# A planner with other prices, and rotary halves exchanged by copies instead of DMAs

## The chip, the cores and the metric

The kernel runs on one core of a Trainium2 chip. The metric is the device time of one execution in microseconds (us). The core has five engines that each work through their own queue in order: TensorE (PE; its weight loads are listed as PEld), VectorE (DVE), ScalarE (ACT), GpSimd (POOL) and SyncE (SP), which here issues nearly all DMAs.

## The reference: what is computed

Two layers of a decoder trunk for one sequence of 512 tokens, model width 1024, in float32. Per layer:

```python
mod = c_silu @ w_ada + b_ada                       # shift, scale, gate
u = rms_norm(x, norm_g) * (1 + scale) + shift
z = u @ w_in                                       # split into 18 column groups
ya = dsa_attention(rope(aq), rope(ak), av, rope(iq), rope(ik), iw) * silu(ag)
yb = swa_sinks_attention(rope(bq), rope(bk), bv, sinks) * silu(bg)
yc = stick_breaking_attention(cq, ck, cv) * silu(cg)
merged = sigmoid(ma)*(ya @ w_br_a) + sigmoid(mb)*(yb @ w_br_b) + sigmoid(mc)*(yc @ w_br_c)
x = x + gate * (merged @ w_out)
```

Mixer A attends to the 128 best keys by an indexer's score, mixer B to a window of 128 tokens, mixer C breaks sticks over all earlier tokens. Heads have 64 channels. The rotary step takes a head's halves x1, x2 (32 channels each) to `[x1*cos - x2*sin, x1*sin + x2*cos]`; it is applied to the queries and keys of A and B and to those of the indexer.

## The kernel before

**Tiles.** Activations lie with channels on the 128 partitions (rows) and the 512 tokens along the row. A projection tile is 128 output channels, that is two heads, by 512 tokens: one PSUM bank, filled by 24 matmuls. Each weight chunk (128x512, tile `wstage`) is split on the chip into a high part `whi` (a cast) and a low part `wlo` (a subtraction), and each activation likewise into `uh` and `ul`; of the four products three are summed, which makes 3 matmuls for each of 8 blocks of the width of 1024. Projection banks are called `ps_z` (three of them), the banks for scores, transposes and mixer outputs `ps_s` (five).

**Phases.** Per layer: a first phase (seven projection tiles, among them the indexer's `ik`, `iq0`, `iq1`), a phase for values with tokens on partitions, then a long middle in which projections, three mixers, gates and branch products are woven together, then the output projection with the next norm. VectorE selects mixer A's keys in the middle phase: 16 rounds of a maximum of eight and a replacement for each of three token blocks, on the tiles `score`. Mixer C runs first, then B, then A; A's first mask addition reads `score`.

**The rotary step** is `rope_evac` (called by `evac` for `iq`, `bq`, `bk`, `aq`, `ak`: 15 tiles per layer). It copies the finished bank z to a tile `zs` in SBUF, has SP issue four DMAs of 32 rows that write the exchanged halves to `m2` (the profile calls it `m`), multiplies z by the cosines into `zc`, multiplies `m2` by the signed sines, and adds. The results `Q` and `KH`/`klow` are then stacked and split for the score matmuls. The key tile of the indexer has a function of its own, `key_and_value`, with the same DMAs.

**Softmax of A and B.** VectorE adds the mask and takes the row maximum in eight operations (`t,mx<-ps_s`, shown as CUSTOM_DVE_ANT_0 in the trace and as ISA in the order), forms the negated maximum `nm`; ScalarE takes exponentials in eight operations with their sums (`den`); the normalised tiles are transposed on TensorE (`ps_s<-small,t`, float32 against the identity).

**What sets the order.** Every operation is first recorded, with the engines that may do it: `cast` may go to ACT, to DVE, and from SBUF to POOL as well; `both` (two tensors) to DVE or, when neither lies in PSUM, to POOL. `Recorder.price` gives each choice a `cost` (how long the engine is held) and a `lag` (until the result is there). `Recorder.forward` is a list scheduler: it gives the next free engine the ready operation with the earliest deadline, keeps a port that DVE and POOL share, hands out buffers, and counts DMAs through one channel. `Recorder.latest` works deadlines back from the end. `order` repeats this five times and keeps the plan that ends first by its own prices. `emit` writes the instructions out in that order, so that each engine's queue is fixed. All instructions are emitted in one helper, which is why nearly every row has the same line (L567 before; L577 in the changed program).

Of the kernel before, what the change touches and what calls it, by code (L numbers as in the profile page):

```python
# [25 lines left out]
F32 = mybir.dt.float32  # L26
F32R = mybir.dt.float32r
BF16 = mybir.dt.bfloat16
# [230 lines left out]
class Recorder:  # L259
    PIPE = 0.17  # L260
    CROSS = 0.055
    ROUNDS = 5

    def __init__(self, tc, nc, psum, sbuf):
# [58 lines left out]
    def price(self, x, engine, op, args, kw):  # L323

        y = Way()
        y.op, y.args, y.kw, y.mode, y.port = op, args, kw, None, False
        o = x.writes[0] if x.writes else None
        if op == "preload_act_table_set":
            y.cost = y.lag = 1.3
            return y  # L330
        if op == "dma_start":
            n = 1
            for d in (o or x.reads[0]).shape:
                n *= d
            y.cost, y.lag, y.mode = 0.35 if engine == "SP" else 0.1, n * 4 / 365e3, "dma"
            return y
        n = 1
        for d in o.shape[1:]:
            n *= d
        from_psum = any(v.tile.pool.name[:3] == "ps_" for v in x.reads)  # L340
        if engine == "PE":
            if op == "pairs":
                w = [q[2].shape[-1] for q in args]
                if args[0][2].dtype == F32:
                    c, y.mode = 0.03 + sum(4 * v / 2.4e3 for v in w[::2]), "c"
                else:
                    c, y.mode = 0.095 + sum(max(0.112, 0.4375e-3 * v + 0.007) for v in w[::2]), "r"
                y.cost, y.lag = c, c + self.PIPE
            elif op == "transpose":
                c, y.mode = 0.109, "t"  # L350
                y.cost, y.lag = c, c + self.PIPE
            else:
                rhs, y.mode = args[2], "m"
                c = 4 * n / 2.4e3 + 0.01 if rhs.dtype == F32 else 0.06 if rhs.dtype == BF16 else 0.4375e-3 * n + 0.007
                y.cost, y.lag = c, c + self.PIPE
            return y
        accum = "accum_out" in kw
        if engine == "ACT":
            b = 0.1 if isinstance(kw.get("bias"), View) or isinstance(kw.get("scale"), View) else 0.0
            c = 0.2 + 0.82e-3 * n + (b if not accum else 0.08) - (0.03 if from_psum else 0)  # L360
        elif engine == "DVE":
            y.port = not from_psum and op not in ("max", "match_replace", "memset", "reciprocal")
            if op == "tensor_tensor_scan":
                c = 1.21
            elif op == "max":
                c = 0.15 + 1.05e-3 * args[1].shape[-1]
            elif op == "match_replace":
                c = 0.145 + 1.05e-3 * args[2].shape[-1]
            elif n <= 16:
                c = 0.2 + (0.1 if accum else 0)  # L370
            elif op == "tensor_tensor_reduce":
                c = 0.147 + 1.05e-3 * n
            elif from_psum:
                c = 0.147 + 1.05e-3 * n + (0.08 if accum else 0)
            elif op in ("tensor_scalar", "tensor_copy"):
                c = 0.2 + 0.45e-3 * n if op == "tensor_scalar" else 0.15 + 0.5e-3 * n
            elif op == "memset":
                c = 0.1 + 0.6e-3 * n
            else:
                c = 0.15 + 1.05e-3 * n + (0.08 if accum else 0)  # L380
        else:
            y.port = n > 16
            if op == "memset":
                c = 0.12 if n < 16 else 0.52
            elif op == "tensor_copy":
                c = 0.2 + 0.82e-3 * n
            elif op == "tensor_scalar":
                c = 0.2 + 2.8e-3 * n
            else:
                c = 0.1 + 2.35e-3 * n  # L390
        y.cost = y.lag = c
        return y


    def forward(self):
        E = {e: {"free": 0.0, "port": 0.0, "mode": None, "ready": {}, "pend": []} for e in self.real}
        dma_free = 0.0
        waiting = {}
        for x in self.list:
            x.left, x.est, x.bound, x.taken = len(x.preds), 0.0, len(x.tiles), False  # L400
# [32 lines left out]
        while len(out) < len(self.list):  # L433
            best = None
            for name, e in E.items():
                free, port, pend, ready = e["free"], e["port"], e["pend"], e["ready"]
                while pend and pend[0][0] <= free + 1e-9:
                    i = heapq.heappop(pend)[1]
                    ready[i] = self.list[i]
                mine = None  # L440
                for i in list(ready):
                    x = ready[i]
                    if x.taken:
                        del ready[i]
                        continue
                    y = x.alts[name]
                    at = max(free, port) if y.port else free
                    if len(x.alts) > 1 and self.elsewhere(x, name, at, E):
                        continue
                    key = (at, x.prio, i)  # L450
                    if mine is None or key < mine:
                        mine = key
                if mine is None or mine[0] > free + 1e-9:
                    while pend and self.list[pend[0][1]].taken:
                        heapq.heappop(pend)
                    if pend:
                        est, i = pend[0]
                        x = self.list[i]
                        at = max(est, port) if x.alts[name].port else est
                        key = (at, x.prio, i)  # L460
                        if (mine is None or key < mine) and not (len(x.alts) > 1 and self.elsewhere(x, name, at, E)):
                            mine = key
                        elif mine is None:
                            mine = None
                if mine is not None:
                    asked = max(free, self.list[mine[2]].est)
                    if best is None or (mine[0], asked, mine) < best[:3]:
                        best = (mine[0], asked, mine, name)
            assert best is not None, "no instruction may go"
            (at, _, i), name = best[2:]  # L470
            e, x = E[name], self.list[i]
            y = x.alts[name]
            x.taken, x.engine = True, name
            e["ready"].pop(i, None)
            hold = y.cost
            if name == "PE":
                if e["mode"] is not None and y.mode != e["mode"]:
                    hold += 0.095 if {"c", "r"} & {y.mode, e["mode"]} else 0.0
                e["mode"] = y.mode
            x.start, x.hold = at, hold  # L480
            e["free"] = at + hold
            if y.port:
                E["POOL"]["port"] = at + hold + (self.CROSS if name == "DVE" else 0.0)
                E["DVE"]["port"] = at + hold
            if y.mode == "dma":
                x.end = dma_free = max(at + 1.9, dma_free) + y.lag
            else:
                x.end = at + y.lag + (hold - y.cost)
            out.append(x)
            for s in x.succs:  # L490
                s.est = max(s.est, x.end + self.between(x, s))
                s.left -= 1
                offer(s)
            for t in x.tiles:
                t.users -= 1
                t.done = max(t.done, x.end + self.CROSS)
                if t.users == 0:
                    heapq.heappush(t.pool.free, (t.done, t.slot))
                    give(t.pool)
        return max(x.end for x in out), out  # L500

    def between(self, x, s):
        if x.engine == "PE" and "PE" in s.alts:
            return x.start - x.end
        return 0.0 if list(s.alts) == [x.engine] and x.alts[x.engine].mode != "dma" else self.CROSS

    def elsewhere(self, x, name, at, E):

# [86 lines left out]
def trunk(ctx, tc, xT, vecs, w_ss, w_gt, w_first, w_t, w_v, w_br, w_o, rope, consts, out):  # L595
# [22 lines left out]
    def t512(tag, bufs=None, dt=F32):  # L618
        return rec.tile(tag, [P, S], dt)
# [213 lines left out]
        st[name] = sigmoid_from(z, t512("sm", 2))  # L833

    def rope_evac(z):
        zs, m2, zc = t512("zs"), t512("m2"), t512("zc")
        cast(zs, z)
        for a, b in ((0, 32), (32, 0), (64, 96), (96, 64)):
            SP.dma_start(m2[a:a + 32], zs[b:b + 32])
        DVE.tensor_tensor(out=zc, in0=z, in1=cos_t, op=OP.mult)  # L840
        both(m2, m2, sin_t, OP.mult)
        both(zc, zc, m2, OP.add)
        return zc
# [712 lines left out]
    for fn, chunks in wv.items:  # L1556
# [4 lines left out]
        args = [ch.get(pos - len(chunks) + i) for i in range(len(chunks))]  # L1561
# [65 lines left out]
```

## Time and profile before

| | |
|---|---|
| median of 3 runs | 1181.32 us (1180.83 to 1181.7) |
| the profiled execution | 1182.6 us, of which the span from first to last instruction is 1180.8 |
| granted TensorE clock | 0.998 |
| PE busy | 1164.9 us, 99% of the span |
| DVE busy | 940.6 us, 80% |
| ACT busy | 563.2 us, 48% |
| POOL busy | 255.5 us, 22% |
| mean DMA rate | 118 GB/s |

How to read it: busy is time in which an engine runs instructions, so the rest of the span is waiting. In a row of a group, the numbers behind the bar are total busy time and the mean in ns of one instruction, then the idle time ahead of its instructions and what ended it. In a row of waits stand the total, the number of times and the longest. Tile names come without buffer numbers.

### The profile page before, as it was taken

The numbers are of one execution on the slowest core, as the hardware profiler recorded it, in microseconds if no ns is written. First come the engines' busy times: TensorE is split into PE (matmuls) and PEld (weight loads), VectorE is DVE, ScalarE is ACT, GpSimd is POOL, SyncE is SP. The second block draws the span as 40 slices with busy tenths as digits, with TensorE's granted clock in tenths as the row PEclk, the third lists the DMA queues.
The fourth block names the chain that finished last, engine by engine and source line by source line (L and its number), as shares of the span: only waits on it lengthen the run. The fifth ranks groups of instructions, "written<-read, shape, count | busy, mean of one in ns | idle before, by whom it ended". The sixth has DMA issues, their size and how long they took to land.

```text
span 1180.8 us, 17862 instructions
## 1 busy us (share of the span) xinstructions
PE 1164.9 (99%) x6006; PEld 967.6 (82%) x6006; DVE 940.6 (80%) x2094; ACT 563.2 (48%) x1171; POOL 255.5 (22%) x297
## 2 busy tenths in 40 slices
PE   9999999999999999999999999999999999999997
PEld 8799777788878887778899987777888788877886
DVE  7867999989888788686476599998897887667754
ACT  6534677653456632642144157665534654235222
POOL 1100455531111101001210016453221011111120
PEclk9999999999999999999999999999999999999999
DMA  9644323344434454344534432234342334322342
GB/s 338 230 115 126 90 72 90 99 119 122 117 105 128 134 144 142 89 138 148 166 113 104 135 97 80 81 88 115 120 125 74 97 83 124 98 65 88 94 128 100
DMA packets 81916, 139.41 MB, mean 118 GB/s; under 512 B 10016, under 2 KB 22560, under 8 KB 81824
## 3 DMA queue, kind: packets, MB, share of 16 engines
q1 hardware_dynamic: 80672, 136.17, 39.4%
q10 hardware_dynamic: 1152, 2.10, 0.5%
q8 instruction: 47, 0.77, 0.3%
q14 instruction: 45, 0.37, 0.1%
HBM read 125.39 MB, written 4.19 MB: 110 GB/s over the span
## 4 chain that ended last, share of the span: by engine, by line
PE 89%; DVE 4%; DMA 3%; ACT 1%; SPq 1%; issue 1%; DVEq 0%; ACTq 0%
PE ps_z L567 68%; PE ps_s L567 16%; PE ps_s L565 5%; DMA wstage<-in_w_first 2%; DVE t L567 1%; SPq L567 1%; ACT t L567 1%; DMA m<-zs 1%; DVE Y L567 0%; DVE wlo L567 0%; DVE Q L567 0%; DVE m L567 0%; DMA wstage<-in_w_ss 0%; DVE zc L567 0%; DVE vc L567 0%
## 5 line engine op out<-in xcount | busy, mean ns | idle before, releaser
L567 PE MATMUL ps_z<-uh,whi 128*128 128x512 f32 (+1 forms) x908 | 356.7, 394 | 2.7 <-DVE xm L567 1.2
L567 PE MATMUL ps_z<-uh,wlo 128*128 128x512 f32 (+1 forms) x908 | 353.3, 389 | 0.0
L567 PE MATMUL ps_z<-ul,whi 128*128 128x512 f32 (+1 forms) x908 | 352.8, 389 | 0.2 <-DVE ul L567 0.2
L567 POOL TENSOR_TENSOR wlo<-wstage,whi 128x512 fp32r<-128x512 f32 (+1 forms) x135 | 172.8, 1281 | 619.2 <-DVE whi L567 312.0
L567 PEld LDWEIGHTS ps_z<-uh,whi 128*128 128x128 f32 x908 | 170.4, 188 | 38.8 <-issue 3.6
L567 PEld LDWEIGHTS ps_z<-uh,wlo 128*128 128x128 f32 x908 | 170.6, 188 | 35.5 <-issue 1.7
L567 PEld LDWEIGHTS ps_z<-ul,whi 128*128 128x128 f32 x908 | 170.8, 188 | 32.6 <-DVE ul L567 0.9
L567 DVE TENSOR_TENSOR wlo<-wstage,whi 128x512 fp32r<-128x512 f32 (+2 forms) x237 | 154.5, 655 | 13.2 <-ACT whi L567 4.9
L567 ACT CAST whi<-wstage 128x512 fp32r<-128x512 f32 (+2 forms) x148 | 87.7, 596 | 153.2 <-PE ps_z L567 103.2
L567 DVE CAST whi<-wstage 128x512 fp32r<-128x512 f32 (+2 forms) x172 | 70.3, 409 | 105.9 <-PE ps_z L567 88.1
L567 PE MATMUL ps_z<-Y,whi 128*128 128x512 f32 x384 | 118.8, 390 | 0.8 <-ACT e L567 0.8
L567 ACT ACTIVATE e<-ps_z 128x512 f32<-128x512 f32 x68 | 40.3, 594 | 124.9 <-PE ps_z L567 124.7
L567 PEld LDWEIGHTS ps_z<-Y,whi 128*128 128x128 f32 x384 | 71.7, 188 | 16.0 <-issue 1.1
L567 ACT ACTIVATE e<-e 128x512 f32<-128x512 f32 x96 | 60.3, 630 | 39.2 <-DVE e L567 38.1
L567 ACT ACTIVATE t<-t 128x512 f32<-128x512 f32 x120 | 71.7, 628 | 8.5 <-POOL t L567 3.4
L567 PE MATMUL ps_z<-Y,wlo 128*128 128x512 f32 x192 | 74.6, 389 | 0.0
L567 ACT ACTIVATE t<-t,nm 128x256 f32<-128x256 f32 (+3 forms) x128 | 65.1, 510 | 16.2 <-DVE nm L567 16.2
L567 POOL CAST whi<-wstage 128x512 fp32r<-128x512 f32 (+2 forms) x52 | 31.4, 605 | 177.9 <-PE ps_z L567 104.3
L567 PE MATMUL ps_s<-small,t 128*128 128x128 f32 x432 | 57.7, 273 | 1.6 <-DVE t L567 0.9
L567 PEld LDWEIGHTS ps_s<-small,t 128*128 128x128 f32 x432 | 50.0, 140 | 10.5 <-ACT t L567 1.6
L567 DVE MAX8 m<-score 128x8 f32<-128x256 f32 (+2 forms) x96 | 53.4, 556 | 1.7
L567 DVE SCALAR_TENSOR_TENSOR wstage<-wstage,csr 128x512 f32<-128x512 f32 x64 | 46.2, 723 | 10.1 <-DMA wstage<-in_w_ss 7.2
(209 smaller groups left out, 2019.6 us busy)
## 6 DMA issues: line engine op xcount, KB each, us to landing
wstage<-in_w_t SPq DMA_DIRECT2D x212, 256.0 KB, 2.7
wstage<-in_w_v SPq DMA_DIRECT2D x48, 182.0 KB, 2.3
Y<-in_w_ss SPq DMA_DIRECT2D x16, 512.0 KB, 6.4
m<-zs SPq DMA_DIRECT2D x128, 64.0 KB, 2.0
wstage<-in_w_gt SPq DMA_DIRECT2D x32, 256.0 KB, 2.7
wstage<-in_w_ss SPq DMA_DIRECT2D x32, 256.0 KB, 2.8
wstage<-in_w_o SPq DMA_DIRECT2D x32, 256.0 KB, 2.7
wstage<-in_w_first SPq DMA_DIRECT2D x16, 256.0 KB, 4.6
```

What stands on the lines that cost most here:

```text
L565: self.real[engine].matmul(*[real(a) for a in q[:3]], start=q[3], stop=True, skip_group_check=True)
L567: made = getattr(self.real[engine], y.op)(*[real(a) for a in y.args], **{k: real(v) for k, v in y.kw.items()})
```

## The change

Two things. First, `rope_evac` has no `zs` and no DMAs any more: four copies of 32 rows read the bank z in PSUM and write `m2` at the exchanged rows. Each may go to ScalarE or VectorE. `key_and_value` stays as it was. Second, the planner's constants are others: how long operations take by engine and shape, how much of one is overlapped by the next on its engine (`OVERLAP`), what TensorE's changes between kinds of matmul cost (`ENTER`), when the port shared by DVE and POOL comes free, how long until a dependent instruction may start (`between`), how long DMAs take to issue and land, and how many may be under way (`LANES`).

```diff
 class Recorder:
     PIPE = 0.17
     CROSS = 0.055
+    NEXT = 0.033
+    LANES = 8
+    OVERLAP = {"PE": 0.0, "ACT": 0.095, "DVE": 0.083, "POOL": 0.06, "SP": 0.0}
+    ENTER = {"m": 0.0, "t": 0.035, "c": 0.17, "r": 0.17}
+    TOPORT = 0.13
...
-            y.cost, y.lag, y.mode = 0.35 if engine == "SP" else 0.1, n * 4 / 365e3, "dma"
+            y.cost, y.lag, y.mode = (0.58 if x.reads and x.writes and not x.reads[0].tile.pool.fixed else 0.36) if engine == "SP" else 0.1, n * 4 / 385e3, "dma"
...
-                c = 4 * n / 2.4e3 + 0.01 if rhs.dtype == F32 else 0.06 if rhs.dtype == BF16 else 0.4375e-3 * n + 0.007
+                c = 4 * n / 2.4e3 + 0.01 if rhs.dtype == F32 else 0.06 if rhs.dtype == BF16 else (n + 33.5) / 2.4e3
...
-            b = 0.1 if isinstance(kw.get("bias"), View) or isinstance(kw.get("scale"), View) else 0.0
-            c = 0.2 + 0.82e-3 * n + (b if not accum else 0.08) - (0.03 if from_psum else 0)
+            b = 0.09 * sum(isinstance(kw.get(k), View) for k in ("bias", "scale"))
+            c = 0.205 + 0.83e-3 * n + (b if not accum else 0.18) - (0.04 if from_psum else 0)
...
             elif op in ("tensor_scalar", "tensor_copy"):
-                c = 0.2 + 0.45e-3 * n if op == "tensor_scalar" else 0.15 + 0.5e-3 * n
+                c = 0.225 + 0.45e-3 * n if op == "tensor_scalar" else 0.16 + 0.52e-3 * n
...
-        y.cost = y.lag = c
+        y.cost, y.lag = c - self.OVERLAP[engine], c
...
                 if e["mode"] is not None and y.mode != e["mode"]:
-                    hold += 0.095 if {"c", "r"} & {y.mode, e["mode"]} else 0.0
+                    hold += self.ENTER[y.mode]
...
             if y.port:
-                E["POOL"]["port"] = at + hold + (self.CROSS if name == "DVE" else 0.0)
-                E["DVE"]["port"] = at + hold
+                E["POOL"]["port"] = at + y.lag + self.CROSS if name == "DVE" else at + hold
+                E["DVE"]["port"] = at + y.lag - self.TOPORT
             if y.mode == "dma":
-                x.end = dma_free = max(at + 1.9, dma_free) + y.lag
+                x.end = dma_free = max(at + 3.0, dma_free) + y.lag * (1.6 if dma_free < 5.5 else 1.0)
+                lanes.append(x.end)
+                if name == "SP" and len(lanes) >= self.LANES:
+                    e["free"] = max(e["free"], lanes[-self.LANES])
...
-        return 0.0 if list(s.alts) == [x.engine] and x.alts[x.engine].mode != "dma" else self.CROSS
+        if x.alts[x.engine].mode == "dma":
+            return self.CROSS
+        return self.NEXT if list(s.alts) == [x.engine] else 0.15 if "PE" in s.alts else 0.07 if list(s.alts) == ["POOL"] else 0.04
...
     def rope_evac(z):
-        zs, m2, zc = t512("zs"), t512("m2"), t512("zc")
-        cast(zs, z)
+        m2, zc = t512("m2"), t512("zc")
         for a, b in ((0, 32), (32, 0), (64, 96), (96, 64)):
-            SP.dma_start(m2[a:a + 32], zs[b:b + 32])
+            cast(m2[a:a + 32], z[b:b + 32])
         DVE.tensor_tensor(out=zc, in0=z, in1=cos_t, op=OP.mult)
```

The other changed prices are of the same kind (matmul pairs, transposes, `match_replace`, very short operations, and 0.06 us more for `scalar_tensor_tensor`).

**The order at three places.** First VectorE around the rotary tile aq0 of layer 0. Here `zc_3693` and `m2_3700` (after the change `zc_3684` and `m2_3676`) are its two tiles, `Q_3758` (`Q_3723`) its result, and the ISA rows are the mask additions of mixer B's last pair. Before:

```order
L567 TENSOR_TENSOR zc_3693<-ps_z_3582,rt_84 128x512
L567 TENSOR_TENSOR Y_3698<-e_3685,Y_3698 128x512
L567 CAST whi_3716<-wstage_3595 128x512
L567 TENSOR_TENSOR wlo_3724<-wstage_3595,whi_3716 128x512
L567 ISA t_3734,mx_3735<-ps_s_3718,cb_85 128x256
L567 ISA mx_3735 128x1
L567 TENSOR_TENSOR m2_3700<-m2_3700,rt_84 128x512
L567 ISA t_3749,mx_3735<-ps_s_3720,cb_85 128x256
```

And in the changed program:

```order
L577 COPY m2_3676<-ps_z_3570 32x512
L577 TENSOR_TENSOR zc_3684<-ps_z_3570,rt_84 128x512
L577 TENSOR_TENSOR Y_3679<-e_3668,Y_3679 128x512
L577 TENSOR_TENSOR m2_3676<-m2_3676,rt_84 128x512
L577 TENSOR_TENSOR wlo_3699<-wstage_3503,whi_3671 128x512
L577 TENSOR_TENSOR zc_3684<-zc_3684,m2_3676 128x512
L577 ISA t_3719,mx_3720<-ps_s_3697,cb_85 128x256
```

The multiplication of `m2` and the sum now stand ahead of the first mask addition; before, the multiplication stood behind it. One of the four copies is on VectorE, the three others stand together on ScalarE.

Second GpSimd's last instructions, which split the weights of layer 1's end. Before:

```order
L567 TENSOR_TENSOR wlo<-wstage,whi 128x512 x6
L567 TENSOR_SCALAR e<-e 128x512
L567 TENSOR_TENSOR wlo<-wstage,whi 128x512
L567 CAST whi<-wstage 128x512
L567 TENSOR_TENSOR wlo<-wstage,whi 128x512 x12
```

And in the changed program:

```order
L577 TENSOR_TENSOR wlo<-wstage,whi 128x512 x2
L577 CAST whi<-wstage 128x512
L577 TENSOR_TENSOR wlo<-wstage,whi 128x512 x2
L577 CAST whi<-wstage 128x512 x2
L577 TENSOR_TENSOR xm_8673<-xm_8673,sm 128x512
L577 TENSOR_SCALAR e<-e 128x512
```

The subtractions of that end have gone to VectorE. Over the program 512-wide `wlo` go from 178 to 236 on VectorE and from 130 to 72 on GpSimd.

Third VectorE in the last update of the residual, with the squares `m` summed for the final norm. Before:

```order
L567 SCALAR_TENSOR_TENSOR xm_12111<-ps_z,mods_77,G 128x256
L567 SCALAR_TENSOR_TENSOR xm_12141<-ps_z,mods_77,G 128x256
L567 TENSOR_SCALAR xm_12111<-xm_12111,small 128x256
L567 TENSOR_TENSOR m_11865<-m_11865,e 128x256
L567 TENSOR_TENSOR t<-xm_11858,ps_s 128x256
```

And in the changed program:

```order
L577 SCALAR_TENSOR_TENSOR xm_12051<-ps_z,mods_77,G 128x256
L577 TENSOR_TENSOR m_11805<-m_11805,e 128x256
L577 SCALAR_TENSOR_TENSOR xm_12081<-ps_z,mods_77,G 128x256
L577 TENSOR_SCALAR xm_12081<-xm_12081,small 128x256
L577 TENSOR_TENSOR t<-xm_11798,ps_s 128x256
```

The sum into `m` has moved ahead of the last update.

More of the change, by code (lines that the diff above doesn't have):

```diff
@@ L344, in price @@
                 if args[0][2].dtype == F32:
-                    c, y.mode = 0.03 + sum(4 * v / 2.4e3 for v in w[::2]), "c"
+                    c, y.mode = 0.21 + sum(4 * v / 2.4e3 for v in w[::2]), "c"
                 else:
-                    c, y.mode = 0.095 + sum(max(0.112, 0.4375e-3 * v + 0.007) for v in w[::2]), "r"
+                    c, y.mode = 0.26 + sum((v + 33) / 2.4e3 for v in w[::2]), "r"
                 y.cost, y.lag = c, c + self.PIPE
             elif op == "transpose":
-                c, y.mode = 0.109, "t"
+                c, y.mode = 0.1085, "t"
                 y.cost, y.lag = c, c + self.PIPE
@@ L367, in price @@
             elif op == "match_replace":
-                c = 0.145 + 1.05e-3 * args[2].shape[-1]
+                c = 0.215 + 1.045e-3 * args[2].shape[-1]
             elif n <= 16:
-                c = 0.2 + (0.1 if accum else 0)
+                c = 0.27 if op == "tensor_scalar" and len(x.reads) > 2 else 0.22 if op == "tensor_scalar" else 0.165 + (0.1 if accum else 0)
             elif op == "tensor_tensor_reduce":
@@ L379, in price @@
             else:
-                c = 0.15 + 1.05e-3 * n + (0.08 if accum else 0)
+                c = 0.15 + 1.05e-3 * n + (0.0 if accum else 0.06 if op == "scalar_tensor_tensor" else 0.0)
         else:
@@ L396, in forward @@
         E = {e: {"free": 0.0, "port": 0.0, "mode": None, "ready": {}, "pend": []} for e in self.real}
-        dma_free = 0.0
+        dma_free, lanes = 0.0, []
         waiting = {}
```

## The prediction, made before the result was known

> **What bounds the kernel now.** I read the page's busy table first, then the chain of waits, then who TensorE waited for.
>
> ```profile
> PE 1164.9 (99%) x6006; PEld 967.6 (82%) x6006; DVE 940.6 (80%) x2094; ACT 563.2 (48%) x1171; POOL 255.5 (22%) x297
> ```
> ```profile
> 399.73 59.87 PE ps_z L567 x264
> ```
> The second row is one piece of the chain: 264 projection matmuls of 128x512 in 59.87 us, 227 ns each, with nothing between them. Busy on PE is therefore real work here, not a pipeline that looks full. The change leaves the count of matmul instructions as it is (5835 in both programs, by the order), so TensorE's own work cannot shrink. What can move is the 15.9 us of the 1180.8 us span in which it is not busy:
>
> ```profile
> PE ps_z L567 <- ACT e L567: 2.0, 2, 1.2
> PE ps_s L567 <- DVE t L567: 1.4, 3, 0.7
> PE ps_z L567 <- DVE xm L567: 1.2, 1, 1.2
> PE ps_s L567 <- DVE m L567: 1.2, 1, 1.2
> PE ps_s L567 <- DVE epst L567: 1.0, 1, 1.0
> PE ps_s L567 <- ACT t L567: 0.6, 1, 0.6
> ...
> ```
> The columns are total us, times, longest. All waits of PE sum to 8.7 us (these 7.4, and 1.3 of the first 70 us, for loads and first tiles). The other 7 us are the tail after PE's last matmul. So a gain is a matter of a few us, and only a loss could be large.
>
> **Which of these waits the rotary exchange makes.** The chain in the stretch of aq0, layer 0, in order of time:
>
> ```profile
> 327.45 0.59 ACT zs L567
> ...
> 328.62 1.43 SPq L567
> ...
> 330.73 2.05 DMA m<-zs
> ...
> 332.80 0.69 DVE m L567
> ...
> 335.16 0.69 DVE Q L567
> 335.84 0.03 issue
> 335.88 0.69 DVE Q L567
> ...
> 337.03 0.34 DVE t L567
> ...
> 338.15 1.97 ACT t L567 x8
> ```
> The copy to zs ends at 328.0; the four DMAs are issued one behind the other on SP and land at 332.8. VectorE, in order, holds the mask additions of a softmax (t) behind m, so ScalarE's exponentials start at 338.15, and PE waits 0.6 us for t. The same road leads to two more waits: in layer 1 bq1's m starts 5.5 us after the end of its zs copy, and PE waits 1.2 us for xm, queued on VectorE behind it; ak0's m starts 4.3 us after its copy, and PE waits 0.7 us for t:
>
> ```profile
> 793.37 0.61 DVE zs L567
> ...
> 799.52 0.69 DVE m L567
> ...
> 912.64 0.59 ACT zs L567
> ...
> 917.55 0.69 DVE m L567
> ```
>
> **The change part by part.**
>
> *The exchange.* Thirty rotary tiles lose one whole copy and four DMAs each and get four 32-row copies from PSUM. By the order, 85 of the 120 copies stand on ScalarE and 35 on VectorE. No 32-row copy from PSUM is in the trace; nearest are
>
> ```profile
> L567 ACT COPY zs<-ps_z 128x512 f32<-128x512 f32 x20 | 11.7, 583 | 22.9 <-PE ps_z L567 19.5 <-DVE zc L567 2.3 <-DMA m<-zs 1.1
> L567 ACT CAST KH<-KH 64x512 fp32r<-64x512 f32 x13 | 8.0, 619 | 0.5
> L567 DVE COPY zs<-ps_z x8: 678/680/692, 61.6 to 989.0; 128x512 f32<-128x512 f32 x8
> ```
> The middle one moves 64 rows to the other half and costs as much as 128 rows of its kind, so I price by row length: 0.583 us on ScalarE, 0.680 on VectorE. The lower bound would be a quarter of these (if rows counted), the upper 0.71 with the 0.03 us gap below. ScalarE: 85 less 21 whole copies, +37 us; VectorE: 35 less 9, +18 us. SP loses 120 issues. Latency: at aq0 and ak0 three copies go to ScalarE and one to VectorE beside them, 1.75 us; bq1 has all four on ScalarE, 2.3 us. From the start of the copy to the start of m it was 5.4, 4.9 and 6.2 us. Each m multiplication comes 3 to 4 us earlier; the PE waits there were 0.6, 0.7 and 1.2 us. They go: **-2.5 us** (bounds -2.5 and 0, if the next input is as late). Next late at the first place are ScalarE's eight exponentials themselves. The added copies on ScalarE are hidden by its 52% of free time; without that cover a tile's evacuation would be up to 4 x 0.58 us and hold its ps_z bank (three exist) that long.
>
> *The plan.* Prices and overlaps in the planner alter which engine takes work and its place on that engine; the matmuls keep nearly their order. The largest shift is the weight split's subtraction:
>
> ```profile
> L567 DVE TENSOR_TENSOR wlo<-wstage,whi 128x512 fp32r<-128x512 f32 x178 | 122.4, 689 | 9.8 <-ACT whi L567 3.1
> L567 DVE CAST whi<-wstage 128x512 fp32r<-128x512 f32 x139 | 58.8, 424 | 83.2 <-PE ps_z L567 70.9 <-PE ps_s L567 8.4 <-DMA wstage<-in_w_first 1.1
> L567 POOL TENSOR_TENSOR wlo<-wstage,whi 128x512 fp32r<-128x512 f32 x130 | 167.9, 1292 | 590.0 <-DVE whi L567 312.0 <-DVE score L567 97.3 <-PE ps_z L567 48.4
> ```
> 178 become 236 on VectorE and 130 become 72 on GpSimd: +58 x 0.689 = +40 us against -58 x 1.292 = -75. With 31 more whi casts (+13) and the copies (+18), VectorE gets about 70 us more, of 240 us free over the span. The free time lies mostly where it waits for PE to give weight buffers back (83.2 us ahead of whi), so at most places this costs nothing. It matters in the selection of keys, from the first replacement of maxima to the first mask of mixer A:
>
> ```profile
> core 0: us, PE busy (x) PEld busy (x) DVE busy (x) ACT busy (x) POOL busy (x), PEclk, DMA share, GB/s
> 115.00:351.80 236.80, 236.19 (x1238) 189.83 (x1237) 216.62 (x501) 140.32 (x293) 85.42 (x108) 1.00 0.35 101
> 690.00:929.00 239.00, 236.99 (x1237) 189.86 (x1237) 215.35 (x498) 140.58 (x292) 84.91 (x106) 1.00 0.34 97
> ```
> ```profile
> L567 DVE TENSOR_SCALAR t<-t,den 128x256 f32<-128x256 f32 x46 | 14.8, 354 | 0.1
> L567 DVE CUSTOM_DVE_ANT_0 t<-ps_s,cb 128x256 f32<-128x256 f32 x48 | 18.0, 418 | 0.2
> ```
> There VectorE is 91 and 90% busy, and the order puts 38 and 34 more instructions on it. On average: 9.5 wlo (+6.5), 8.5 whi (+3.6), 7.5 copies (+5.1), 6 operations of 64 rows at 0.7 us (+4.2), 7 normalisations of t fewer (-2.5): +17 us, some 16 after overlap. It would then be 98 and 97% busy. Waits that need not return are those for the exchange (m<-zs) and for weight buffers (whi<-PE):
>
> ```profile
> DVE whi L567 <- PE ps_z L567: 3.5, 4, 1.3
> DVE m L567 <- DMA m<-zs: 2.6, 2, 1.3
> ...
> DVE zc L567 <- ACT zs L567: 1.4, 3, 0.6
> ...
> ```
> ```profile
> DVE whi L567 <- PE ps_z L567: 4.5, 5, 1.5
> DVE m L567 <- DMA m<-zs: 4.4, 4, 1.5
> ...
> ```
> (layer 0, then layer 1, which has the same 1.4 us for zc). That fits, barely. New PE waits: lower bound 0, upper 17.8 us (worked out under rival B). A selection round may slide without harm as long as mixer A's mask is in time, so I take a value near the low end, **+1.5 us**.
>
> The plan now takes 0.083 us from every VectorE operation for overlap with the one before. The chain above shows both kinds: t, 0.418 us long by its group, follows at steps of 0.34, but each 64-row Q starts 0.03 us after the end of its forerunner. [...]
>
> PE's remaining mid-program waits (ACT e 2.0, and 0.7 of DVE t) come from other late inputs. A plan with nearer durations should remove some; bounds 0 and -2.7, I take two thirds, **-1.8**. The start keeps its transfers in nearly the same order: 0 (bounds 0 and -1.3). At the end the order puts the product m<-m,e ahead of the last xm update:
>
> ```profile
> 1172.18 0.42 ACT L567 ACTIVATE e<-xm 128x256 f32<-128x256 f32 x1 [0.96 <-DVE xm L567]
> 1172.80 0.70 PE L567 MATMUL ps_s<-m,nones 128*128 128x256 f32 x2 [1.17 <-DVE m L567]
> 1173.33 0.59 PE L567 MATMUL ps_s<-e,nones 128*128 128x256 f32 x2
> ```
> Then only e (ready at 1172.60) is late and its matmul starts near 1172.8 instead of 1173.33: **-0.5** (bounds -0.6 and 0).
>
> Sum: -2.5 + 1.5 - 1.8 - 0.5 = -3.3 us. The profiled execution took 1182.6 us, a span of 1180.8 and 1.8 around it, so it would take 1179.3; it lies 1.3 above the median of the runs, 1181.32. Against the median: **1178.0 us**.
>
> **The rivals.**
>
> *A*, the forecast, 1178.0 (1176 to 1181): 0.44.
>
> *B, VectorE becomes the bound in the selection of keys.* For it: 98%, and the 0.03 us gaps at changes of rows, 0.22 us per copy against what is planned, 1.8 us in each stretch. Against it: its waits shrink when work is queued. Layer 0 needs 216.6 + 16 + 1.8 = 234.4 of 236.8 us. If all its idle time stays but that for the exchange (2.6 for m, 1.4 for zc) and for buffers (3.5), 12.7 us, it is 10.3 us over; layer 1, likewise (215.4 + 16 + 1.8 + 13.3 against 239), 7.5: together 17.8. It decides once more than 2.4 us of idle per stretch must stay. Half of the excess with the gains for exchange and tail: 1181.3 - 3.0 + 8.9 = 1187 us. 0.25.
>
> *C, nearly all mid-program waits go* (8.7 less 1.0 at the first matmul and 0.7 of the last): 1174.3 us. For it: each is a single late input of at most 1.2 us. Against: the order of PE hardly alters, so the same chains stay tight. 0.18.
>
> *D, the exchange was hidden anyway*, the next input being as late: only the tail is left, 1180.8 us. For it: at the first place the exponentials follow in a chain of their own. 0.13. That the copies are not exchanged at all is excluded by the order: SP keeps 8 of 128 DMAs to m.
>
> **How the numbers follow.** The predicted time is A's. A measurement of this kernel tells about 0.2% from no change: 2.4 us, so faster is below 1179.0 and slower above 1183.7. A gives faster 0.32 and same 0.12; C faster 0.18; D same 0.13; B slower 0.20 and same 0.05. Faster 0.50, same 0.30, slower 0.20. The range, 1173 to 1188, takes in C and the middle of B; A's own is 1176 to 1181.
>
> **What would show it.** Right: no DMA to m but for the key tile, the 32-row copies at 0.58 and 0.68 us, no PE wait left behind m at the three places, VectorE near 86% of the span. B: VectorE over 97% in the two stretches and PE idle for t, Q or whi there. D: the three waits still there under another name. Wrong altogether would be a 32-row copy far from 0.6 us, or PE's busy time altered by more than 2 us.

## The result and the profile after

The changed program takes **1192.1 us** (median of 5 runs, 1191.4 to 1193.0) against 1181.7 of the kernel before on the same chip: ratio 1.009, 95% interval 1.0078 to 1.0101. It is 10 us slower; forecast were 1178 us, and 1187 for the rival in which VectorE falls behind. Of all executions in this document two stand apart, one of a later version at 2359 us and one of the kernel before at 3003 us; the ratios leave them out. The profiled execution took 1192.4 us, a span of 1190.6, 9.8 us longer than before.

The busy table on the page of the profile, after:

```profile
PE 1170.0 (98%) x6006; PEld 969.6 (81%) x6006; DVE 993.0 (83%) x2262; ACT 572.0 (48%) x1195; POOL 150.2 (13%) x195
```

TensorE's idle time in the span went from 15.9 to 20.6 us (+4.7), and its busy time, with the same 6006 matmul records, grew by 5.1. Together they are the 9.8 us. Who TensorE waited for, after (total us, times, longest):

```profile
PE ps_s L577 <- DVE t L577: 10.5, 14, 3.4
PE ps_s L577 <- DVE epst L577: 1.0, 1, 1.0
PE ps_s L577 <- DMA wstage<-in_w_first: 1.0, 1, 1.0
PE ps_s L577 <- DVE vc L577: 0.6, 1, 0.6
PE ps_s L577 <- ACT e L577: 0.2, 1, 0.2
```

The late inputs of before (ScalarE's e, 2.0 us; xm and m, 1.2 each) have all but gone. In their place TensorE waits 14 times for a tile `t` that VectorE has not yet written. The selection of keys, again from the first replacement to the first mask of mixer A, now lasts 244.1 us (236.8 before) and 241.3 (239.0 before). In the columns of the windows shown before:

```profile
117.00:361.10 244.10, 238.17 (x1231) 190.61 (x1230) 228.33 (x538) 143.33 (x304) 60.58 (x78) 0.99 0.31 90
701.70:943.00 241.30, 236.94 (x1235) 189.22 (x1234) 227.42 (x531) 143.52 (x304) 59.73 (x77) 1.00 0.31 88
```

TensorE idles 5.9 us in the first (0.6 before) and 4.4 in the second (2.0 before). VectorE is late but not full: 93.5 and 94.2%. So where does its time go? First the copies themselves, from the view of the tile `m` (count, then min/median/max in ns):

```profile
L577 ACT COPY m<-ps_z x79: 575/578/582, 64.1 to 1003.7; 32x512 f32<-32x512 f32 x79
L577 DVE COPY m<-ps_z x33: 679/684/696, 197.5 to 1001.8; 32x512 f32<-32x512 f32 x33
```

They cost what a whole copy costs, as was assumed. What was not assumed is who waits for whom. VectorE's and then ScalarE's waits for the other engine at these tiles, after:

```profile
DVE m L577 <- ACT m L577: 11.8, 18, 1.2
DVE zc L577 <- ACT m L577: 7.2, 12, 1.1
```
```profile
ACT m L577 <- DVE m L577: 19.6, 19, 2.4
ACT m L577 <- DVE zc L577: 13.9, 11, 2.9
```

A copy on ScalarE waits until VectorE's copy from the same bank has ended, `zc` on VectorE (also a read of that bank) waits for ScalarE's copy, and so on: the two engines **take turns at the bank**. None of ScalarE's 79 copies overlaps in time with any of VectorE's 61 reads of `ps_z` by `m` and `zc`. The two rows of VectorE are 19.0 us; 1.3 of them are waits of m's multiplication, which needs the copies in any case, so 17.7 us are turns. That the four copies write one tile is not what makes them wait: a little later both engines write the two halves of one tile `Q` at the same time.

```profile
335.89 0.62 ACT L577 CAST Q<-zc 64x512 fp32r<-64x512 f32 x1 [1.32 <-DVE zc L577]
...
336.23 0.42 DVE L577 CAST Q<-zc 64x512 fp32r<-64x512 f32 x1
```

What the copies and `zc` have in common is the bank. The kernel itself records no dependency between two reads, yet the waits are in the trace; no run here leaves them out. Before the change VectorE lost as much to the DMAs:

```profile
DVE m L567 <- DMA m<-zs: 19.7, 17, 2.3
...
DVE zc L567 <- ACT zs L567: 3.2, 7, 0.6
```

So the change did not free VectorE; it put one wait in the place of another. The chain in the stretch of aq0, layer 0, after, up to the longest wait of TensorE:

```profile
330.70 0.71 DVE m L577
...
331.43 0.59 ACT m L577
...
332.04 0.70 DVE zc L577
...
333.35 0.58 ACT m L577
...
333.96 0.69 DVE m L577
...
336.23 0.42 DVE Q L577
336.65 0.03 issue
336.69 0.42 DVE t L577
337.12 0.03 issue
337.15 0.70 DVE Q L577
...
347.11 0.36 DVE t L577
347.48 0.04 issue
347.52 1.76 PE ps_s L577 x7
```

The first four copies and `zc` go back and forth, and m's multiplication starts at 333.96, 3.3 us after the first copy (5.4 before the change, 1.75 forecast). The next rotary tile does the same from 340.08 (copies on VectorE and ScalarE, then `zc`). In between, each change between `Q` (64 rows) and `t` (128 rows) has the 0.03 us gap that the prediction had read off; the new plan expects an overlap of 0.083 there. Counted over all of VectorE's rows, two neighbours of 128 rows overlap by 0.082 us at the median, and where either has 64 or 32 rows there is a gap of 0.031. Some 260 such places without a wait, at 0.031 us of gap and 0.083 of overlap that is not there (a few do overlap), add up to some 25 us that the plan leaves out, 7.6 and 7.2 us of it in the two stretches. TensorE stands still for 3.4 us before 347.52, and then runs on at half speed:

```profile
335.00:343.00 8.00, 8.00 (x37) 6.64 (x37) 7.05 (x25) 2.68 (x5) 2.55 (x2) 1.00 0.26 73
347.50:352.50 5.00, 4.98 (x17) 4.16 (x18) 4.85 (x14) 2.20 (x6) 0.00 (x0) 0.50 0.04 15
```

The granted clock (third column from the end) is 0.50 in these 5 us, in which 17 matmuls run. By that clock they cost an estimated 2.5 us more, which show as busy time, not as waiting. That is half of the 5.1 us by which TensorE's busy time grew; the other half can't be put down to single rows.

### The profile page after: what moved, and what is told of

It is laid out like the page before. It is cut to its first block, busy times and chain, and to the rows that moved or that the text cites. A ratio compares the mean times of both kernels' runs of the same rounds, so it can differ in the third digit from the quotient of the medians.

```text
span 1190.6 us, 17620 instructions
## 1 busy us (share of the span) xinstructions
PE 1170.0 (98%) x6006; PEld 969.6 (81%) x6006; DVE 993.0 (83%) x2262; ACT 572.0 (48%) x1195; POOL 150.2 (13%) x195
## 4 chain that ended last, share of the span: by engine, by line
PE 79%; DVE 15%; issue 3%; ACT 2%; DMA 1%; SPq 0%; DVEq 0%; ACTq 0%
PE ps_z L577 59%; PE ps_s L577 16%; DVE t L577 6%; PE ps_s L575 4%; DVE m L577 2%; DVE score L577 2%; DVE Q L577 1%; DVE wlo L577 1%; DVE KH L577 1%; ACT m L577 1%; ACT t L577 1%; DVE klow L577 1%; DVE zc L577 1%; DMA vc<-in_xT 1%; DVE whi L577 0%
## 5 line engine op out<-in xcount | busy, mean ns | idle before, releaser
L577 DVE TENSOR_TENSOR wlo<-wstage,whi 128x512 fp32r<-128x512 f32 (+2 forms) x296 | 193.4, 656 | 13.0 <-ACT whi L577 3.6
L577 DVE CAST whi<-wstage 128x512 fp32r<-128x512 f32 (+2 forms) x213 | 86.9, 409 | 89.8 <-PE ps_z L577 73.8
L577 POOL TENSOR_TENSOR wlo<-wstage,whi 128x512 fp32r<-128x512 f32 (+2 forms) x76 | 96.8, 1277 | 507.5 <-PE ps_z L577 102.9
L577 ACT CAST whi<-wstage 128x512 fp32r<-128x512 f32 (+2 forms) x112 | 66.6, 599 | 83.1 <-PE ps_z L577 68.7
L577 ACT ACTIVATE t<-t 128x512 f32<-128x512 f32 x120 | 68.7, 625 | 10.1 <-DVE t L577 9.2
L577 PE MATMUL ps_s<-small,t 128*128 128x128 f32 x432 | 59.6, 279 | 10.6 <-DVE t L577 10.5
L577 ACT COPY m<-ps_z 32x512 f32<-32x512 f32 x79 | 45.7, 578 | 45.9 <-DVE m L577 19.6
L577 PE MATMUL ps_s<-KH,Q 128*128 128x256 f32 (+3 forms) x280 | 52.5, 309 | 0.2
```

What stands on the lines that cost most here:

```text
L577: made = getattr(self.real[engine], y.op)(*[real(a) for a in y.args], **{k: real(v) for k, v in y.kw.items()})
```

## The experiments

Two suspects, then: the turns at a bank (**T**), and the gaps at changes of rows (**H**, for held). Rivals: VectorE simply has too much work (**O**), the plan has lost slack, wherever it lay (**S**), or some other new price does it (**P**). Each ratio is to the kernel before on the same chip, with its 95% interval. Edits are against the changed program.

**One part alone.** First the new plan with the old exchange by DMA:

```diff
-        m2, zc = t512("m2"), t512("zc")
+        zs, m2, zc = t512("zs"), t512("m2"), t512("zc")
+        cast(zs, z)
-            cast(m2[a:a + 32], z[b:b + 32])
+            SP.dma_start(m2[a:a + 32], zs[b:b + 32])
```

> The changed planner with the old exchange (one whole copy and four DMAs per rotary tile). Theory T, turns: the loss comes from the exchange, since the four copies and the cosine product read one PSUM bank and the trace of the change shows ScalarE and VectorE waiting for each other there (VectorE 11.8 + 7.2 us for ScalarE's m, ScalarE 19.6 + 13.9 us for VectorE's m and zc), which the plan does not count. Then this run is near or below the kernel before: 1176 to 1183 us. Theory O, overbooked: the loss comes from the planner, which takes 0.083 us of overlap from every VectorE operation and moves 58 subtractions from GpSimd to VectorE. Then this run is as slow as the change, 1187 to 1194 us, with PE waiting for t on VectorE about 10 us.

Then the old planner (all prices and rules of before) with the new exchange:

> The old planner with the new exchange. T: slower than before, 1186 to 1194 us, with the same mutual waits of ScalarE and VectorE at m and zc. O: the old planner keeps VectorE some 8% freer, so the exchange costs nothing: 1177 to 1183 us.

Measured: the plan alone 1181.4 us, ratio 1.0001 [0.9991, 1.0010], as T expected; the copies alone 1182.3, 1.0008 [0.9998, 1.0017], as O expected. Neither costs anything; only **both together** do. VectorE's waits with the copies alone:

```profile
DVE m L567 <- ACT m L567: 14.1, 22, 1.2
DVE zc L567 <- ACT m L567: 11.5, 20, 0.9
```

25.6 us, some 24 of them turns: more than in the changed program, and no loss. The old plan charges each VectorE instruction its full duration, so it keeps room. With the new plan alone VectorE is as busy as after the change (988.1 us, 84%), fuller in the two stretches (96.5 and 95.5%), and no time is lost, which speaks against O. Nor do the gaps alone explain the loss: that program has some 21 us of them, just as unplanned. What it lacks is the turns. VectorE waits nowhere for the DMAs to `m` there, and 2.2 us for the copy `zs`:

```profile
694.60:931.30 236.70, 235.05 (x1230) 188.10 (x1228) 226.05 (x536) 133.19 (x286) 48.66 (x67) 1.00 0.33 97
```
```profile
DVE zc L577 <- ACT zs L577: 2.2, 6, 0.4
```

**All copies on ScalarE**, `ACT.copy(...)` in place of `cast(...)`:

> The change, with the four copies bound to ScalarE, so that a bank changes hands at most once, before or after the cosine product; VectorE loses 35 copies, 24 us. T: most of the mutual waits go, 1180 to 1186 us. O: VectorE is freer by 2% of the span, so also faster than the change, but the unplanned overlap remains: 1185 to 1190 us.

1187.3 us, 1.0049 [1.0034, 1.0063]: half of the loss goes. That lies in O's range and outside T's. `zc` and the copies still alternate, and VectorE also has 9.4 us less work, so this run does not part the two.

**Turns in the plan.** The planner keeps, for each PSUM tile, when each engine's last use ends, and lets a read by the other start 0.04 us after it:

```diff
+    def bank(self, x, name):
+        return max((u + 0.04 for t in x.tiles if t.pool.name[:3] == "ps_" for e, u in t.use.items() if e != name), default=0.0) if name != "PE" else 0.0
...
-                    at = max(free, port) if y.port else free
+                    at = max(max(free, port) if y.port else free, self.bank(x, name))
```

> The change, with one thing added to the planner: a read of a PSUM tile by ScalarE or VectorE may start only 0.04 us after the other engine's last read of it has ended. T: the turns are now in the plan, work is put into the gaps, and most of the loss goes: 1178 to 1184 us, with VectorE waiting for ScalarE's m less than 8 us instead of 19. O: the overbooking is untouched: 1188 to 1193 us.

1184.0 us, 1.0021 [1.0012, 1.0031]: 8 of the 10 us come back, though VectorE is about as busy as in the changed program (989.9 us, 84%) and the gaps are still unplanned. T's two signs hold, the time at the edge of its range (1178 to 1184) and VectorE's waits for ScalarE's m, 4.6 us where under 8 were expected:

```profile
DVE zc L582 <- ACT m L582: 4.6, 4, 1.3
```

**No overlap for VectorE** (0.0 for 0.083):

> The change with the planner's overlap for VectorE set from 0.083 us to 0, as the old planner had it; all other prices new. The first runs: planner alone 1.0001, exchange alone 1.0008, both 1.009 of before, so neither causes the loss by itself. Theory S, slack: the mutual waits at the bank (25 us of VectorE even with the old planner) cost nothing while the plan holds VectorE longer than it is held, and fall on PE once 0.083 us is taken from each of some 2000 operations. Then this run loses little, 1181 to 1186 us, with the mutual waits still there. Rival P, other prices: it is the shift of work to VectorE and the new places that hurt, through prices other than the overlap; then 1188 to 1193 us.

1181.6 us, 1.0007 [0.9997, 1.0016]. With this one constant undone the loss is gone, all other new prices in place, so P falls. The price of 0 gives VectorE 0.083 us of room at each instruction, some 190 us in all, and so speaks for S as much as for H and T; VectorE still waits 28.9 us for ScalarE's copies, at no loss.

**Gaps in the plan.** An instruction of other than 128 rows gets no overlap and 0.11 us on top, for its own gap and that of the next one; 178 instructions at 0.193 us are 34 us, somewhat more than the 25 counted:

```diff
-        y.cost, y.lag = c - self.OVERLAP[engine], c
+        y.cost, y.lag = c - self.OVERLAP[engine] if engine != "DVE" or o.shape[0] == P else c + 0.11, c
```

> The change, with the planner told that a VectorE operation on fewer than 128 rows has no overlap and costs 0.11 us more than its duration (the 0.03 us gap ahead of it and the overlap that its follower loses). Theory H, holds: unplanned gaps at changes of rows (35 copies and some 110 operations of 64 rows, together about 15 us of VectorE) make the loss: 1181 to 1186 us. Theory T, turns: they are a small part, 1188 to 1192 us.

1177.6 us, 0.9970 [0.9960, 0.9979], better than H expected. TensorE's waits, and VectorE's for the copies:

```profile
PE ps_s L577 <- DVE epst L577: 1.0, 1, 1.0
PE ps_s L577 <- ACT t L577: 0.7, 1, 0.7
PE ps_s L577 <- DVE t L577: 0.2, 1, 0.2
```
```profile
DVE m L577 <- ACT m L577: 14.7, 22, 1.2
DVE zc L577 <- ACT m L577: 7.1, 11, 1.2
```

The waits for t fall from 10.5 to 0.2 us, while VectorE's turns stay as long (21.8 us, less 4.5 of m's multiplication: 17.3, as in the changed program). The price also moves work: VectorE is 26.5 us less busy (966.5 for 993.0) and ScalarE 26.9 more, and 16 of the copies from ps_z are on VectorE instead of 33. How much of the gain is the room at the gaps and how much the lighter VectorE isn't separated here. At the rotary tile of the same place all four copies now stand on ScalarE, one behind the other, in the chain of this version:

```profile
333.96 0.58 ACT m L577
...
334.55 0.58 ACT m L577
...
335.14 0.58 ACT m L577
...
335.73 0.58 ACT m L577
```

**The same room, spread evenly.** Overlap 0.067 for 0.083 on every VectorE instruction, 0.016 x 2262 = 36 us in all:

> A control for the gap prices (which brought 1192.1 to 1177.6 us): the change with the overlap of every VectorE operation at 0.067 instead of 0.083 us. 0.016 us on each of some 2080 operations is 33 us of planned VectorE time, as much as 0.193 us on the 178 operations of fewer than 128 rows, but spread evenly. If any slack of that size does it (S): 1176 to 1181 us. If it must stand where the gaps are (H): 1184 to 1190 us.

1197.2 us, 1.0138 [1.0122, 1.0155]: slower still, and outside the ranges of both S and H. S as a mere total falls; it matters where the plan puts the time. A price of the same size on 178 other instructions was not run, so it isn't shown that the place must be the gaps. And **more overlap**, 0.099:

> The dose the other way: the change with an overlap of 0.099 us, more than the 0.08 that the trace shows, so that about 33 us more of VectorE is left out of the plan. If lateness of VectorE against its plan is the cause, this is slower than the change: 1197 to 1215 us, with more of PE's time spent waiting for t on VectorE. If the change's loss has to do with the particular places of some operations, no trend: 1183 to 1193 us.

1202.5 us, 1.0181 [1.0166, 1.0196]: in the range of the first theory. But TensorE's waits for VectorE's t, 10.0 us, did not grow as it expected; it waits longer for other tiles (4.4 us for ScalarE's t).

**Which rows.** The gap price for 32-row instructions alone, and for 64-row ones alone:

> The change with the gap price for the 32-row copies alone (35 on VectorE). If the copies are the mis-priced part: 1177 to 1181 us. If the 64-row operations weigh more (about 110 to 140 of them): 1184 to 1190 us.

> The change with the gap price for the operations of 64 rows alone. If these weigh more: 1177 to 1181 us. If the copies are the mis-priced part: 1186 to 1192 us.

1186.6 us, 1.0047 [1.0032, 1.0062], and 1180.0 us, 0.9990 [0.9981, 0.9999], both as expected if the 64-row ones weigh more. Of the gap price, the part for the stacked `Q` and `KH` parts of 64 rows, whose code the change did not touch, does most.

**Both prices**, with the copies and with the DMAs:

> The change with both additions to the planner, the turns at a bank and the gaps at changes of rows. With the turns alone it took 1184.0 us. H: 1179 to 1182 us. T: 1183 to 1185 us.

> The changed planner with the old exchange by DMAs and both additions, the turns at a bank (there the copy to zs and the cosine product) and the gaps at changes of rows. Planner alone took 1181.4 us. If what remains of PE's waits comes from unplanned gaps and turns: 1177 to 1180 us. If it comes from elsewhere: 1180 to 1183 us.

1177.5 us, 0.9971 [0.9959, 0.9983], a little better than either theory expected, and 1178.3 us, 0.9977 [0.9967, 0.9986], as expected if gaps and turns are what is left. With both in the plan, no difference between copies and DMAs can be told.

A way to read these runs, argued and not shown: gaps and turns take VectorE's time alike, and what counts is what the plan leaves out of both. That is 25 + 18 us in the changed program, which loses 10; 24 + 5 with the turns priced, which loses 3; 21 + 2 with the plan alone, which loses nothing; and with the gaps priced 17 us of turns, which gains 3.5.

**Is it luck of one plan?** The overlaps 0, 0.067, 0.083 and 0.099 gave 1181.6, 1197.2, 1192.1 and 1202.5 us: not in order of the overlap, and 0.067 fits no sum of that kind. So neighbours, 0.080 and 0.086, were run of three versions: the change, the change with the gap price, and with both prices.

> The change with the planner's overlap of VectorE at 0.080 instead of 0.083 us for every operation, row changes included. H (unplanned gaps at changes of rows make the loss): the gaps stay unplanned, so the time stays well above the kernel before, 1186 to 1203 us. Scatter (a small move of any price moves the plan's luck by 10 us): anything from 1176 to 1200, overlapping with the runs in which the gaps are priced.

> The change with the planner's overlap of VectorE at 0.086 instead of 0.083 us. H: 1186 to 1203 us, as with 0.083. Scatter: anything from 1176 to 1200.

> The version that prices an operation of other than 128 rows at 0.11 us more and without overlap (1177.6 us), with the overlap at 0.080 us. H: 1176 to 1181 us, and PE's waits for VectorE's t under 2 us. Scatter: anything from 1176 to 1200.

> The same with the overlap at 0.086 us. H: 1176 to 1181 us. Scatter: anything from 1176 to 1200.

> The version with both prices (row changes and turns at a bank, 1177.5 us) with VectorE's overlap at 0.080 instead of 0.083 us. If both prices are right and what is left is the plan's scatter of some 4 us: 1176 to 1182 us, and DVE's waits for ScalarE's m under 8 us. If the gain over the kernel before was the luck of one plan: 1181 to 1184 us, as with the two neighbours of the version with the first price alone (1182.0 and 1182.2).

> The same with the overlap at 0.086 us: right prices 1176 to 1182 us, luck of one plan 1181 to 1184 us.

| overlap | 0.080 | 0.083 | 0.086 |
|---|---|---|---|
| the change | 1191.7 | 1192.1 | 1192.9 |
| gaps priced | 1182.0 | 1177.6 | 1182.2 |
| gaps and turns priced | 1178.3 | 1177.5 | 1177.9 |

The change lies clear of the two others in all three columns: between 0.080 and 0.086 the loss belongs to the unpriced program, not to one plan. With the gap price alone the plan scatters by 4.6 us, and its two neighbours (1.0006 [0.9997, 1.0016] and 1.0008 [0.9999, 1.0018]) only draw level with the kernel before, a little outside what H expected (1176 to 1181). With both prices three plans of three are 0.3% faster: 0.9973 [0.9963, 0.9983], 0.9971, 0.9972 [0.9961, 0.9984]. The waits say why. TensorE's for t, in the two neighbours of the change, then VectorE's turns in the neighbour 0.080 with both prices:

```profile
PE ps_s L577 <- DVE t L577: 9.4, 14, 1.6
```
```profile
PE ps_s L577 <- DVE t L577: 8.1, 10, 1.6
```
```profile
DVE zc L582 <- ACT m L582: 4.6, 5, 1.3
```

There, at 0.080, the planner by itself puts 103 of the 112 copies from ps_z on ScalarE, and VectorE's turns are short (4.6 us in place of 17.7).

What stays open: why the even reductions land where they do, 1197 at 0.067 and 1182 at 0. A plan that is wrong at a few hundred places has no smooth answer to one constant, but that is argued, not shown.

## Why the prediction was wrong, by its steps

- **What bounds the kernel: right.** TensorE does, "a gain is a matter of a few us, and only a loss could be large". The best versions here gain 3 to 4 us. But TensorE's busy time was taken as fixed; it grew by 5.1 us, where the prediction had named 2 us as a sign of being wrong altogether.
- **Price of the copies: right.** 0.583 and 0.680 us were taken; 578 and 684 ns were measured.
- **Latency of the exchange: wrong.** The words "three copies go to ScalarE and one to VectorE beside them, 1.75 us" took the two engines to read one bank side by side. They take turns, and it took 3.3 us. The trace of before had shown it: `zc` waited 3.2 us in seven places for ScalarE's copy `zs`, although both only read the bank. This program has two kinds of these waits: between `zc`, which reads all 128 rows, and a copy of 32 (the rows of waits for or by `zc`, 7.2 and 13.9 us), and between two copies, which read different rows (the other two, 11.8 and 19.6 us, with 1.3 of m's multiplication). Whether either kind could be left out, no run here shows.
- **-2.5 for the three waits behind the exchange: wrong as a sum.** The wait for xm is gone, but at aq0 the 0.6 us for t became 3.4, and the t waits in all went from 1.4 to 10.5 us.
- **-1.8 for the remaining mid-program waits: right in size.** It counted e and 0.7 us of t; the t waits grew, but ScalarE's e went from 2.0 to 0.2 us, and by the new prices: with the plan alone it is 0.2, with the copies alone still 2.0.
- **-0.5 for the tail: right.** From the start of TensorE's last projection matmul to the end of the span it was 9.45 us before (1171.35 to 1180.8) and 8.94 after (1181.66 to 1190.6).
- **+1.5 for new waits: the step that failed.** It lay "near the low end" of 0 to 17.8. Measured are 9.1 us more of waiting for t and an estimated 2.5 us of half clock behind the longest wait. Two sizes went into it wrongly. The gaps at changes of rows were counted for the 35 copies alone, 1.8 us in each stretch; but the plan takes the overlap from the 143 instructions of 64 rows as well, and with them the gaps are 7.6 and 7.2 us. The `Q` rows that showed this were quoted in the prediction. And the waits for the exchange, 2.6 and 4.4 us for m and 1.4 for `zc` in each stretch, were struck out as waits that "need not return", when turns of 5.0 and 5.1 us came in their place. That these two together are the cause rests on the runs in which pricing either one brought most of the loss back.
- **Rival B had the direction and the victim, not the form.** Its test was VectorE over 97% in both stretches; it is at 93.5 and 94.2% (the page of the profile gives 83% of the span where 86% was forecast), and the work added in a stretch is 12 us where some 16 were counted. VectorE is late because it waits and pauses where the plan has it working, not because it is full. B's own point of decision, more than 2.4 us of idle that must stay in each stretch, was passed: 15.8 and 13.9 us stayed. That B's middle, 1187 us, comes nearest to the measured time is in part luck.
- **Gaps at changes of rows: right in kind, sized too low.** 32-row copies show them too, which no row of before could tell: 0.031 us from 32 to 128 rows and 0.032 the other way. The 0.22 us per copy in rival B, some 8 us over the program, was an estimate from the `Q` rows, a gap of 0.03 us and a missing overlap of 0.083 on either side; no run of before shows it for a copy. With the 64-row instructions the trace after has some 25.

## What to carry to other kernels

A planner's price that is right on average but wrong for one kind of instruction can cost most where the engine has little room: a price that is too high hides what isn't modelled (gaps, turns), and lowering it everywhere uncovers all of it at once. Before an overlap is taken from every instruction, look for the rows that show none, and price those. When a wait is removed from a tile, ask who else reads its bank: in this program two engines that read one PSUM bank work by turns (17.7 us of VectorE's waits, and 3.3 us from the first copy to m's multiplication where 1.75 was forecast), so splitting the reads of one bank over both brings less than the plan expects.

## What the hardware showed that was not expected

A short stop of TensorE can cost more than its own length: here 3.42 us of waiting and an estimated 2.7 us behind it. After the last matmul before the long wait had ended at 344.1, the clock stayed at 1.00 for two microseconds and then fell, and came back late. Two slices of the changed program:

```profile
346.00:347.00 1.00, 0.00 (x0) 0.00 (x0) 0.94 (x3) 1.00 (x5) 0.00 (x0) 0.55 0.57 66
352.00:353.00 1.00, 1.00 (x6) 0.93 (x5) 0.99 (x3) 0.00 (x0) 0.00 (x0) 0.53 0.00 0
```

A mean of 0.55 in the first means half clock from 346.1 on, and 0.53 in the second half clock until 352.9: 6.8 us, after 2.0 us of idling. In the version with overlap 0.099 a wait of 2.30 us was enough, and one of 2.10 us was not; the clock stayed at 1.00 through it:

```profile
350.15 1.31 PE L577 MATMUL ps_s<-small,t 128*128 128x128 f32 x7 [2.10 <-ACT t L577]
...
937.39 1.76 PE L577 MATMUL ps_s<-small,t 128*128 128x128 f32 x7 [2.30 <-ACT t L577]
```
```profile
350.00:351.00 1.00, 0.84 (x5) 0.54 (x5) 1.00 (x5) 1.00 (x5) 0.00 (x0) 1.00 0.04 12
937.00:938.00 1.00, 0.61 (x3) 0.53 (x4) 1.00 (x5) 1.00 (x6) 0.00 (x0) 0.52 0.00 0
940.00:941.00 1.00, 1.00 (x6) 0.77 (x5) 0.95 (x4) 0.66 (x2) 0.00 (x0) 0.77 0.00 0
```

Half clock from 937.0 to 940.5, 3.4 us. A wait of 1.36 us at 930 in the changed program left the clock at 1.00. The length of a wait does not decide alone: where the clock fell, TensorE had idled for 2.01 us (344.10 to 346.11) and 1.95 us (935.09 to 937.04), less than the 2.10 us through which it stayed. The distances between changes of the clock in the two traces are 6.83 us (346.11 to 352.94) and 832.85 (from there to the fall at 1185.79) in the changed program, and 3.41 (937.04 to 940.45) in the version with 0.099: 2, 244 and 1 times 3.4133 us. Whether the clock can change only in such steps, and whether that is why the wait of 2.10 us passed, is not shown; these are too few cases for a threshold.

So in the sum of a prediction for this kernel a wait of about 2 us or more may carry more than itself: by the matmul time that lies in the half-clock stretches, 5.4 and 3.1 us, an estimated 2.7 and 1.5 us more.
